# Batched 64x64 matmul: all of `a` loaded as fp32 through SyncE's queue, cast on VectorE

## The chip, the core and the metric

The kernel runs on one core of one Trainium2 chip. The metric is device time in microseconds (us); lower is better. The core has five engines that matter here: TensorE (PE, matrix products and transposes), VectorE (DVE), ScalarE (ACT), GpSimd (POOL) and SyncE (SP, which here only issues transfers). Sixteen DMA engines move data between the chip's memory (HBM) and the on-chip buffer SBUF. They are fed by queues, and three queues carry this kernel's data: `q0` takes what GpSimd issues, `q1` what SyncE issues, `q10` what ScalarE issues.

## The reference

```python
def setup_inputs():
    return {"a": np.random.randn(1024, 64, 64).astype(np.float32),
            "b": np.random.randn(1024, 64, 64).astype(np.float32)}

def reference(a, b):
    return np.matmul(a, b).astype(np.float32)
```

There are 1024 independent products of 64x64 matrices. Each of `a`, `b` and the output is 16 MiB of fp32, so the least traffic to HBM is 48 MiB.

## The kernel before

**Units of work.** The kernel walks over `a` in 8 slabs `s` of 128 matrices (2 MiB each) and over `b` and the output in 16 blocks `t` of 64 matrices (1 MiB each). Slab `s` serves the blocks `t = 2s` and `t = 2s + 1`; two successive blocks are called a pair below.

**What happens to a slab of `a`.** `load_a` brings it in as four quarters `h`, in each of which a partition holds a contiguous run of 1024 numbers (4 KB of fp32 in HBM). In the kernel before, quarters 0 to 2 go through GpSimd's queue, which turns them into bf16 on the way (the tile `a_sb` is bf16). Quarter 3 goes through SyncE's queue as fp32 into `a_raw`. `regroup` then writes one bf16 tile `a_bf`: line 108 reorders the three bf16 quarters, line 111 casts the fp32 one, both on VectorE. Slab 0 is different (`load_first_a`): its quarters are loaded as fp32, two on SyncE and two on ScalarE, into two borrowed output tiles, and cast by VectorE and ScalarE in turn (line 105). `transpose` turns `a_bf` on TensorE, moving pairs of bf16 as one fp32, and ScalarE copies the result into `at_sb` (line 123).

**What happens to a block.** `spread` (line 133) makes four VectorE copies from `at_sb` into a block-diagonal tile `at_bd`. `cast` (line 144) turns `b` into bf16, on VectorE except for block 0 (ScalarE) and the last block (both, lines 149 and 151). `multiply` runs 64 matmuls (line 189), and `evacuate` copies the result from PSUM to `o_sb` (line 177): eight copies on ScalarE for an even block, six on ScalarE and two on VectorE for an odd one. `store` sends the 1 MiB out (line 166), on GpSimd's queue for blocks 0 to 13, on SyncE's and ScalarE's for the last two.

**Order.** The schedule is written by hand; each engine works through its own instructions in the order of the program, and a queue's transfers go in the order of issue. Iteration `t` of the main loop does `spread(t+1)`, `cast(t+1)`, `load_b(t+3)`, for even `t` from 2 to 6 `load_a(t/2+4)`, then `multiply(t)`, and for even `t` the `regroup` of slab `t/2+2`. `load_b` uses SyncE for even blocks and ScalarE for odd ones:

```python
            if t + B_AHEAD < n_t:
                load_b(t + B_AHEAD)
            if half == 0 and 0 < s < n_s - 1 - A_AHEAD:
                load_a(s + 1 + A_AHEAD)
```

Slabs 1 to 4 are requested before or during iteration 0, and slabs 5, 6, 7 in iterations 2, 4 and 6. There are three buffers each for `a_sb`, `a_raw` and `b_sb` (`A_AHEAD`, `B_AHEAD`), so a load waits until the tile three before it has been consumed; there are eight for `o_sb`.

Of the kernel before, what the change touches and what calls it, by code (L numbers as in the profile page):

```python
# [8 lines left out]
fp32 = mybir.dt.float32  # L9
bf16 = mybir.dt.bfloat16  # L10
# [3 lines left out]
def kernel(  # L14
# [14 lines left out]
    nc = tc.nc  # L29
    B, M, K = a.shape  # L30
    _, _, N = b.shape
# [8 lines left out]
    a_v = a.rearrange("(s g h) (mp v) k -> s h g mp (v k)", h=4, g=32, v=16)  # L40
# [4 lines left out]
    a_pool = ctx.enter_context(tc.tile_pool(name="a_pool", bufs=A_AHEAD))  # L45
    b_pool = ctx.enter_context(tc.tile_pool(name="b_pool", bufs=B_AHEAD))
    work = ctx.enter_context(tc.tile_pool(name="work", bufs=2))
    o_pool = ctx.enter_context(tc.tile_pool(name="o_pool", bufs=8))
    t_psum = ctx.enter_context(
        tc.tile_pool(name="t_psum", bufs=4, space=bass.MemoryType.PSUM)  # L50
    )
# [9 lines left out]
    a_tiles, b_tiles, abf_tiles, at_tiles, bbf_tiles = {}, {}, {}, {}, {}  # L61
# [6 lines left out]

    def load_a(s):

        a_sb = a_pool.tile([128, 3, 16, 64], bf16, name="a_sb")
        for h in range(3):
            nc.gpsimd.dma_start(  # L73
                out=a_sb[:, h, :, :].rearrange("p v k -> p (v k)"), in_=a_v[s, h], single_packet=True
            )
        a_raw = a_pool.tile([128, 16, 64], fp32, name="a_raw")
        nc.sync.dma_start(out=a_raw[:].rearrange("p v k -> p (v k)"), in_=a_v[s, 3])  # L77
        a_tiles[s] = a_sb, a_raw

    def load_first_a():  # L80

        raw = [
            o_pool.tile([128, 8, 2, 2, 64], fp32, name="o_sb")[:].rearrange(
                "p gh j wl n -> p (gh j wl n)"
            )
            for _ in range(2)
        ]
        parts = [raw[h % 2][:, 1024 * (h // 2) : 1024 * (h // 2) + 1024] for h in range(4)]
        for h in range(4):
            (nc.scalar if h % 2 else nc.sync).dma_start(out=parts[h], in_=a_v[0, h])  # L90
        a_tiles[0] = parts

    def load_b(t):
        b_sb = b_pool.tile([128, 16, 128], fp32, name="b_sb")
        queue = nc.scalar if t % 2 else nc.sync
        queue.dma_start(out=b_sb[:], in_=b_v[t])  # L96
        b_tiles[t] = b_sb

    def regroup(s):
        a_sb = a_tiles.pop(s)  # L100
        a_bf = work.tile([128, 16, 4, 64], bf16, name="a_bf")
        if s == 0:
            for h in range(4):
                copy = nc.scalar.copy if h % 2 else nc.vector.tensor_copy
                copy(a_bf[:, :, h, :], a_sb[h].rearrange("p (v k) -> p v k", v=16))  # L105
        else:
            cast_sb, raw = a_sb
            nc.vector.tensor_copy(  # L108
                a_bf[:, :, 0:3, :], cast_sb[:].rearrange("p h v k -> p v h k")
            )  # L110
            nc.vector.tensor_copy(a_bf[:, :, 3, :], raw[:])  # L111
        abf_tiles[s] = a_bf
        at_tiles[s] = work.tile([128, 2, 32, 2, 4, 4], fp32, name="at_sb")

    def transpose(s, j):
        a_cols = abf_tiles[s][:].rearrange("p v h k -> p v (h k)").bitcast(fp32)
        for wl in range(2):
            at_ps = t_psum.tile([128, 4, 128], fp32, name="at_ps")
            for vo in range(4):
                nc.tensor.transpose(  # L120
                    at_ps[:, vo, :], a_cols[:, 4 * vo + 2 * j + wl, :], identity[:]
                )
            nc.scalar.copy(  # L123
                at_tiles[s][:, j, :, wl, :, :],
                at_ps[:].rearrange("p vo (g mp) -> p g mp vo", mp=4),
            )

    def spread(t):
        half = slice(16 * (t % 2), 16 * (t % 2) + 16)
        bd = bd_tiles[t % N_BD]  # L130
        for h in range(4):
            rows = slice(32 * h, 32 * h + 32)
            nc.vector.tensor_copy(  # L133
                bd[rows, :, :, :, h, :].rearrange("p j g wl mo -> p j (g wl) mo"),
                at_tiles[t // 2][rows, :, half, :, :, :].rearrange(
                    "p j g wl mp vo -> p j (g wl) (mp vo)"
                ),
            )

    def cast(t):  # L140
        b_bf = work.tile([128, 16, 128], bf16, name="b_bf")
        b_sb = b_tiles.pop(t)
        if t < n_t - 1:
            (nc.vector.tensor_copy if t else nc.scalar.copy)(b_bf[:], b_sb[:])  # L144
        else:
            for gq in range(4):
                rows = slice(4 * gq, 4 * gq + 4)
                if gq % 2:
                    nc.vector.tensor_copy(b_bf[:, rows, :], b_sb[:, rows, :])
                else:  # L150
                    nc.scalar.copy(b_bf[:, rows, :], b_sb[:, rows, :])  # L151
        bbf_tiles[t] = b_bf

    def store(t):
        for piece in held.pop(t):
            piece()
# [51 lines left out]
            held[t] = [lambda q=q: put(q, 8 if whole else 4) for q in ([0] if whole else [0, 4])]  # L208

    with tc.manual_schedule():  # L210
        load_first_a()

        nc.vector.memset(warm[:, 0:1], 0.0)
        nc.scalar.copy(warm[:, 1:2], warm[:, 0:1])  # L214
        load_b(0)
        load_b(1)
        nc.vector.memset(bd_tiles[0][:], 0.0)  # L217
        make_identity(nc, identity)
        nc.gpsimd.memset(bd_tiles[1][:, 0], 0.0)
        load_a(1)  # L220
        load_b(2)
        nc.gpsimd.memset(bd_tiles[1][:, 1], 0.0)
        load_a(2)
        regroup(0)
        transpose(0, 0)
        transpose(0, 1)
        spread(0)
        cast(0)
        for t in range(n_t):
            s, half = t // 2, t % 2  # L230
            if t + 1 < n_t:
                spread(t + 1)
                cast(t + 1)
# [4 lines that stand above are left out]
            if half == 0 and 0 < s < n_s - 1:  # L238
                transpose(s + 1, 1)
            multiply(t)  # L240
            if t == 0:
                regroup(1)
                load_a(A_AHEAD)
                load_a(A_AHEAD + 1)
                transpose(1, 0)
                transpose(1, 1)
            elif t == 1:
                regroup(2)
            elif half == 0 and s + 2 < n_s:
                regroup(s + 2)  # L250
            if half == 1 and s + 2 < n_s:
                transpose(s + 2, 0)
            if t >= HOLD - 1:
                store(t - HOLD + 1)
        for t in range(n_t - HOLD + 1, n_t):
            store(t)
# [30 lines left out]
```

## Time and profile before

| | |
|---|---|
| runs, median (lowest to highest) | 135.07 us (134.95 to 135.22), 3 runs |
| profiled execution: span from its first to its last instruction | 133.4 us |
| what lies around the span (median less span) | 1.7 us |
| VectorE busy | 94.6 us, 71% |
| ScalarE busy | 87.9 us, 66% |
| TensorE busy (matmul) | 64.4 us, 48% |
| GpSimd busy | 33.0 us, 25% |
| HBM read and written | 33.55 + 16.78 MB, 377 GB/s over the span |

The profiled execution has no separate clocking; its own time is its span of 133.4 us and the 1.7 us around it that the runs show. The profile gives busy times per engine, the span cut into 40 equal slices, the load of each DMA queue, the chain of work that ended last (followed back from the last instruction), and groups of instructions by source line with their number, busy time and mean duration. The GB/s of the DMA views count bytes as they are written at the destination: a quarter that is turned into bf16 on the way counts half of what was read for it. The last line of the table counts the bytes at HBM.

### The profile page before, as it was taken

What the parts mean: (1) busy time and instruction counts of PE and PEld (TensorE: products, weight loads), DVE (VectorE), ACT (ScalarE), POOL (GpSimd) and SP (SyncE); (2) the same over time, 40 slices, a digit from 0 to 9 for tenths busy, and PEclk for the clock granted to TensorE, in tenths of its full rate; (3) what the DMA queues carried; (4) which work ended last, traced back from release to release, by engine and by line L of the source; (5) the groups of instructions that cost most, each with busy time, mean ns of one, the idle gap of its engine ahead of it and who ended that gap; (6) DMA issues with size and microseconds to landing.
All of it is one profiled execution on the core that took longest, in us unless ns stands there. A gap on an engine that the chain in (4) does not pass through costs nothing.

```text
span 133.4 us, 2837 instructions
## 1 busy us (share of the span) xinstructions
PE 64.4 (48%) x1152; PEld 61.1 (46%) x1152; DVE 94.6 (71%) x120; ACT 87.9 (66%) x161; POOL 33.0 (25%) x43
## 2 busy tenths in 40 slices
PE   0006406960089384289518970956197363970000
PEld 0006306950089274189418950945196363960000
DVE  5930399109998809995999699959999995987000
ACT  3225424999036998969595969696968969099600
POOL 8991000420090070341233021203020410300000
PEclk9999975797557999856985699599959955599555
DMA  3999999999999999999999999999999999999990
GB/s 77 371 329 311 307 311 281 284 306 325 327 312 401 316 320 333 399 384 397 311 281 375 406 389 351 304 316 390 394 396 387 396 392 391 402 405 398 382 319 18
DMA packets 19021, 45.01 MB, mean 337 GB/s; under 512 B 1088, under 2 KB 3136, under 8 KB 19008
## 3 DMA queue, kind: packets, MB, share of 16 engines
q0 software_dynamic: 6832, 20.19, 50.1%
q1 hardware_dynamic: 7120, 14.68, 30.4%
q10 hardware_dynamic: 5056, 9.96, 19.7%
q8 instruction: 9, 0.15, 0.4%
q14 instruction: 4, 0.03, 0.1%
HBM read 33.55 MB, written 16.78 MB: 377 GB/s over the span
## 4 chain that ended last, share of the span: by engine, by line
DMA 53%; DVE 15%; ACT 13%; PE 6%; issue 5%; SPq 2%; DVEq 0%; ACTq 0%
DMA b_sb<-in_b_dram 53%; ACT o_sb L177 9%; DVE at_bd L133 6%; PE o_ps L189 4%; DVE b_bf L144 4%; DVE o_sb L177 3%; PE at_ps L120 2%; ACT at_sb L123 2%; ACT b_bf L144 1%; SPq L90 1%; DVE a_bf L108 1%; SPq L96 1%; ACT b_bf L151 1%; DVE a_bf L111 0%; SPq L77 0%
## 5 line engine op out<-in xcount | busy, mean ns | idle before, releaser
L177 ACT COPY o_sb<-o_ps 64x512 f32<-64x512 f32 x106 | 61.5, 580 | 10.3 <-PE o_ps L189 9.0
L189 PEld LDWEIGHTS <-at_bd 128*128 128x128 bf16 x1024 | 42.3, 113 | 39.5 <-DVE b_bf L144 25.7
L189 PE MATMUL o_ps<-b_bf,at_bd 128*128 128x64 bf16 x960 | 42.6, 216 | 35.4 <-DVE b_bf L144 23.4
L133 DVE COPY at_bd<-at_sb 32x1024 f32<-32x1024 f32 x64 | 46.9, 733 | 14.1 <-ACT at_sb L123 11.8
L120 PE MATMUL at_ps<-identity,a_bf 128*128 128x128 f32 x128 | 21.2, 335 | 19.4 <-ACT a_bf L105 11.2
L166 POOL DMA_DIRECT2D out_dram<-o_sb x14 | 15.4, 1097 | 56.9 <-ACT at_sb L123 23.4
L120 PEld LDWEIGHTS at_ps<-identity,a_bf 128*128 128x128 f32 x128 | 19.3, 180 | 19.5 <-issue 19.5
L123 ACT COPY at_sb<-at_ps 128x512 f32<-128x512 f32 x32 | 17.5, 590 | 11.0 <-PE at_ps L120 7.8
L144 DVE CAST b_bf<-b_sb 128x2048 bf16<-128x2048 f32 x14 | 17.8, 1271 | 9.6 <-DMA b_sb<-in_b_dram 9.4
L73 POOL DMA_DIRECT2D a_sb<-in_a_dram x21 | 13.6, 662 | 26.4 <-DVE a_bf L108 19.4
L177 DVE COPY o_sb<-o_ps 64x512 f32<-64x512 f32 x14 | 9.7, 690 | 0.3
L108 DVE COPY a_bf<-a_sb 128x3072 bf16<-128x3072 bf16 x7 | 6.7, 950 | 0.0
L105 ACT CAST a_bf<-o_sb 128x1024 bf16<-128x1024 f32 x2 | 2.1, 1044 | 5.2 <-DMA o_sb<-in_a_dram 5.2
L111 DVE CAST a_bf<-a_raw 128x1024 bf16<-128x1024 f32 x7 | 4.8, 683 | 0.0
L144 ACT CAST b_bf<-b_sb 128x2048 bf16<-128x2048 f32 x1 | 1.9, 1900 | 3.9 <-DMA b_sb<-in_b_dram 3.9
L105 DVE CAST a_bf<-o_sb 128x1024 bf16<-128x1024 f32 x2 | 2.8, 1382 | 1.9 <-DMA o_sb<-in_a_dram 1.9
L217 DVE MEMSET at_bd<- 128x4096 f32 x1 | 3.5, 3472 | 0.8 <-issue 0.8
L177 DVE COPY o_sb<-at_ps 64x256 f32<-64x256 f32 x8 | 3.4, 422 | 0.5 <-PE at_ps L189 0.4
L151 ACT CAST b_bf<-b_sb 128x512 bf16<-128x512 f32 x2 | 1.1, 615 | 3.6 <-DMA b_sb<-in_b_dram 3.6
L177 ACT COPY o_sb<-at_ps 64x256 f32<-64x256 f32 x8 | 2.9, 366 | 0.1
L214 ACT ACT_TABLE_LOAD x1 | 1.3, 1283 | 2.3 <-issue 2.3
L189 PE MATMUL at_ps<-b_bf,at_bd 128*128 128x64 bf16 x64 | 2.0, 193 | 1.0 <-DVE at_bd L133 1.0
(12 smaller groups left out, 6.1 us busy)
## 6 DMA issues: line engine op xcount, KB each, us to landing
out_dram<-o_sb POOLq DMA_DIRECT2D x14, 1024.0 KB, 21.6
a_sb<-in_a_dram POOLq DMA_DIRECT2D x21, 256.0 KB, 16.4
a_raw<-in_a_dram SPq DMA_DIRECT2D x7, 512.0 KB, 18.7
o_sb<-in_a_dram SPq DMA_DIRECT2D x2, 512.0 KB, 5.9
o_sb<-in_a_dram ACTq DMA_DIRECT2D x2, 512.0 KB, 7.1
out_dram<-o_sb SPq DMA_DIRECT2D x2, 512.0 KB, 7.5
out_dram<-o_sb SPq DMA_DIRECT2D x2, 256.0 KB, 7.8
out_dram<-o_sb ACTq DMA_DIRECT2D x2, 256.0 KB, 5.5
```

What stands on the lines that cost most here:

```text
L73: nc.gpsimd.dma_start(out=a_sb[:, h, :, :].rearrange("p v k -> p (v k)"), in_=a_v[s, h], single_packet=True)
L105: copy(a_bf[:, :, h, :], a_sb[h].rearrange("p (v k) -> p v k", v=16))
L108: nc.vector.tensor_copy(a_bf[:, :, 0:3, :], cast_sb[:].rearrange("p h v k -> p v h k"))
L111: nc.vector.tensor_copy(a_bf[:, :, 3, :], raw[:])
L120: nc.tensor.transpose(at_ps[:, vo, :], a_cols[:, 4 * vo + 2 * j + wl, :], identity[:])
L123: nc.scalar.copy(at_tiles[s][:, j, :, wl, :, :], at_ps[:].rearrange("p vo (g mp) -> p g mp vo", mp=4),)
L133: nc.vector.tensor_copy(bd[rows, :, :, :, h, :].rearrange("p j g wl mo -> p j (g wl) mo"), at_tiles[t // 2][rows, :, half, :, :, :].rearrange(
L144: (nc.vector.tensor_copy if t else nc.scalar.copy)(b_bf[:], b_sb[:])
L166: store_queue(t, lo).dma_start(out=o_v[t, :, lo : lo + n, :], in_=o_sb[:, lo : lo + n].rearrange("p gh j wl n -> p (gh j wl n)"),)
L177: copies[2 * par + wl](dst, src)
L189: nc.tensor.matmul(o_ps[:, gl, g % 2, j, :], at_bd[:, j, g, :, u], b_bf[:, g, 64 * u : 64 * u + 64], start=(u == 0), stop=(u == 1),)
L217: nc.vector.memset(bd_tiles[0][:], 0.0)
```

## The change

All four quarters of every slab are loaded as fp32 into one tile of 4 x 16 x 64 numbers per partition. SyncE issues all of them, except that for slab 0 the odd quarters stay with ScalarE. Slab 0 uses the same pool of three buffers as the others instead of borrowed output tiles. `regroup` of slabs 1 to 7 is one VectorE instruction that reorders and casts 4096 numbers per partition; slab 0 is cast as it was. GpSimd issues stores alone. As the tile of `a` grows from 10 KB to 16 KB per partition, the output pool goes from eight buffers to seven.

```diff
-    o_pool = ctx.enter_context(tc.tile_pool(name="o_pool", bufs=8))
+    o_pool = ctx.enter_context(tc.tile_pool(name="o_pool", bufs=7))
...
     def load_a(s):
 
-        a_sb = a_pool.tile([128, 3, 16, 64], bf16, name="a_sb")
-        for h in range(3):
-            nc.gpsimd.dma_start(
-                out=a_sb[:, h, :, :].rearrange("p v k -> p (v k)"), in_=a_v[s, h], single_packet=True
-            )
-        a_raw = a_pool.tile([128, 16, 64], fp32, name="a_raw")
-        nc.sync.dma_start(out=a_raw[:].rearrange("p v k -> p (v k)"), in_=a_v[s, 3])
-        a_tiles[s] = a_sb, a_raw
-
-    def load_first_a():
...
-        for h in range(4):
-            (nc.scalar if h % 2 else nc.sync).dma_start(out=parts[h], in_=a_v[0, h])
-        a_tiles[0] = parts
+        a_sb = a_pool.tile([128, 4, 16, 64], fp32, name="a_sb")
+        for h in range(4):
+            queue = nc.scalar if s == 0 and h % 2 else nc.sync
+            queue.dma_start(out=a_sb[:, h, :, :].rearrange("p v k -> p (v k)"), in_=a_v[s, h])
+        a_tiles[s] = a_sb
...
-                copy(a_bf[:, :, h, :], a_sb[h].rearrange("p (v k) -> p v k", v=16))
+                copy(a_bf[:, :, h, :], a_sb[:, h, :, :])
         else:
-            cast_sb, raw = a_sb
-            nc.vector.tensor_copy(
-                a_bf[:, :, 0:3, :], cast_sb[:].rearrange("p h v k -> p v h k")
-            )
-            nc.vector.tensor_copy(a_bf[:, :, 3, :], raw[:])
+            nc.vector.tensor_copy(a_bf[:], a_sb[:].rearrange("p h v k -> p v h k"))
...
-        load_first_a()
+        load_a(0)
```

More of the change, by code (lines that the diff above doesn't have):

```diff
@@ L69, in load_a @@
     def load_a(s):
-        a_sb = a_pool.tile([128, 3, 16, 64], bf16, name="a_sb")
-        for h in range(3):
-            nc.gpsimd.dma_start(
-                out=a_sb[:, h, :, :].rearrange("p v k -> p (v k)"), in_=a_v[s, h], single_packet=True
-            )
-        a_raw = a_pool.tile([128, 16, 64], fp32, name="a_raw")
-        nc.sync.dma_start(out=a_raw[:].rearrange("p v k -> p (v k)"), in_=a_v[s, 3])
-        a_tiles[s] = a_sb, a_raw
-    def load_first_a():
-        raw = [
-            o_pool.tile([128, 8, 2, 2, 64], fp32, name="o_sb")[:].rearrange(
-                "p gh j wl n -> p (gh j wl n)"
-            )
-            for _ in range(2)
-        ]
-        parts = [raw[h % 2][:, 1024 * (h // 2) : 1024 * (h // 2) + 1024] for h in range(4)]
+        a_sb = a_pool.tile([128, 4, 16, 64], fp32, name="a_sb")
         for h in range(4):
-            (nc.scalar if h % 2 else nc.sync).dma_start(out=parts[h], in_=a_v[0, h])
-        a_tiles[0] = parts
+            queue = nc.scalar if s == 0 and h % 2 else nc.sync
+            queue.dma_start(out=a_sb[:, h, :, :].rearrange("p v k -> p (v k)"), in_=a_v[s, h])
+        a_tiles[s] = a_sb
     def load_b(t):
@@ L104, in regroup @@
                 copy = nc.scalar.copy if h % 2 else nc.vector.tensor_copy
-                copy(a_bf[:, :, h, :], a_sb[h].rearrange("p (v k) -> p v k", v=16))
+                copy(a_bf[:, :, h, :], a_sb[:, h, :, :])
         else:
-            cast_sb, raw = a_sb
-            nc.vector.tensor_copy(
-                a_bf[:, :, 0:3, :], cast_sb[:].rearrange("p h v k -> p v h k")
-            )
-            nc.vector.tensor_copy(a_bf[:, :, 3, :], raw[:])
+            nc.vector.tensor_copy(a_bf[:], a_sb[:].rearrange("p h v k -> p v h k"))
         abf_tiles[s] = a_bf
```

## The prediction

> **What bounds the kernel now.** I read the page's slices and queues first, then the chain, then the DMA view of two windows, then VectorE's timeline.
>
> ```profile
> DMA  3999999999999999999999999999999999999990
> GB/s 77 371 329 311 307 311 281 284 306 325 327 312 401 316 320 333 399 384 397 311 281 375 406 389 351 304 316 390 394 396 387 396 392 391 402 405 398 382 319 18
> ...
> HBM read 33.55 MB, written 16.78 MB: 377 GB/s over the span
> ...
> DMA 53%; DVE 15%; ACT 13%; PE 6%; issue 5%; SPq 2%; DVEq 0%; ACTq 0%
> ```
>
> The DMA engines are full from the second slice to the last but one, no compute engine is (VectorE 71%), and over half of the chain that ended last is loads of `b`. The GB/s dip to 300 only where casting loads run, as their bytes count half. The DMA view from 0 to 89 us, when the load of block 10 of `b` has just landed, shows this:
>
> ```profile
> q0 software_dynamic: 4337, 10.68, 47.4%
> q1 hardware_dynamic: 4535, 11.16, 34.8%
> q10 hardware_dynamic: 3328, 7.11, 20.9%
> ```
>
> The columns are packets, MB written and share. A casting packet writes 2 KB for 4 KB read and a store's carries 4 KB. Some 26 transfers had finished on q0, each with 16 marker packets, so about 3920 packets hold 10.68 MB: 2630 casting (10.3 MiB read) and 1290 store packets (5.0 MiB). q1 holds 4.5 MiB of fp32 `a` (two quarters of slab 0, seven `a_raw`) and 6.1 MiB of `b`; q10 holds 1 MiB of `a` and 5.8 of `b`. That makes `a` 15.8, `b` 11.9, stores 5.0: 32.7 MiB in HBM bytes. Transfers start near 2.4 us, so a MiB takes (89 - 2.4)/32.7 = 2.65 us, whatever the mixture: from 100 to 111 us, without any `a`, 4.32 MB written take 11 us, or 2.67 us per MiB. **Rule A: N MiB have moved at 2.4 + 2.65 N.** All 48 give 129.6 us; the present kernel's transfers end near 131. So at most 1.5 us can be won, and order is all the change can spoil.
>
> GpSimd had issued nine stores by 89 us (the ninth at 84.2) and five MiB had landed. The page says the same:
>
> ```profile
> out_dram<-o_sb POOLq DMA_DIRECT2D x14, 1024.0 KB, 21.6
> ```
>
> A store needs 21.6 us to land because it shares q0 with the casting loads. **Four MiB of stores stand aside while loads pass, and are paid at the end, beside the last blocks' computing.** How queues share is in the DMA view from 100 to 111 us, where all three have work nearly throughout:
>
> ```profile
> q0 software_dynamic: 608, 2.34, 55.2%
> q1 hardware_dynamic: 525, 1.04, 24.8%
> q10 hardware_dynamic: 463, 0.92, 22.6%
> ```
>
> Packets come out nearly one for one; with 4 KB packets on q0 and 2 KB of `b` on the others, q0 gets over half of the bytes. Last, VectorE's timeline over one pair and the end:
>
> ```profile
> 83.10 0.95 DVE L108 COPY a_bf<-a_sb 128x3072 bf16<-128x3072 bf16 x1
> 83.97 0.68 DVE L111 CAST a_bf<-a_raw 128x1024 bf16<-128x1024 f32 x1
> ...
> 89.08 1.23 DVE L144 CAST b_bf<-b_sb 128x2048 bf16<-128x2048 f32 x1 [1.31 <-DMA b_sb<-in_b_dram]
> ...
> 96.02 0.95 DVE L108 COPY a_bf<-a_sb 128x3072 bf16<-128x3072 bf16 x1
> ...
> 112.33 1.23 DVE L144 CAST b_bf<-b_sb 128x2048 bf16<-128x2048 f32 x1 [1.47 <-DMA b_sb<-in_b_dram]
> ...
> 115.01 3.09 DVE L133 COPY at_bd<-at_sb 32x1024 f32<-32x1024 f32 x4
> ```
>
> A pair takes 96.02 - 83.10 = 12.9 us, of which VectorE waits 1.3 for an even block of `b` (SyncE's). It is nearly full where it matters, though 71% overall.
>
> **The change, part by part.**
>
> *Regroup.* Before: 22.32 to 23.87 us, 1.55 us for both lines. After: one cast of 4096 numbers. L144 takes 1.23 us for 2048, L111 0.68 for 1024, hence 2.45 to 2.75; L108 shows that the reordered reading is not slower, so I take 2.5: +0.95 us a slab, 6.7 us over seven. Six fall where VectorE waits for `b` anyway (below); slab 7's lies on the end.
>
> *GpSimd.* 21 issues (13.6 us) go. GpSimd is 25% busy, so this is worth nothing itself. Ten of the 16 groups of four `at_bd` copies take 3.1 to 3.2 us rather than 2.83; all ten overlap store issues, which stay. One output buffer less: bound by stores in flight, which become fewer; 0.
>
> *Bytes.* HBM bytes stay. Rule A held at 2.65 with casting and 2.67 without, so fp32 may cost 0.02 x 10.5 MiB = 0.2 us, at most; 0.
>
> *Start.* Before, the first block of `b` lands at 19.26 us, behind casting loads. After, only 2 MiB of slab 0 and block 1 share with it: 2.4 + 4 x 2.65 = 13. The first product moves from 21.2 to about 16.5 us (spread(0), now 15.45 to 18.3, ends some 1.8 earlier as slab 0 arrives without competition). That is no gain at the end, since rule A governs the next arrivals; it makes stores start earlier.
>
> *Queues: the main term.* SyncE now issues 28 quarters instead of 7 for slabs 1 to 7, and its queue is a line: slab 4 stands ahead of block 4 of `b`, slab 5 ahead of 6, slab 6 ahead of 8, slab 7 ahead of 10. SyncE also waits for a free `a` buffer with the next even `b` behind it, but these buffers (slab 7 needs regroup(4), near 57 us) are free before the line gets there. Stores have q0 alone. With 4 KB packets on q0 and q1 and 2 KB on q10 their turn is 4/10 of the bytes; a pair needs 2 MiB of stores out of 6, 33%. So stores no longer fall behind; each goes out soon after it is made, in front of loads that computing waits for.
>
> Block 4 of `b` lands when slabs 0 to 4 (10), blocks 0 to 4 (5), some 0.7 of block 5 and the first 2.7 stores have moved: 18.4 MiB, 51.2 us; before 50.2. From there each pair must move all its 6 MiB, 15.9 us, where VectorE needs 12.9 - 1.3 + 0.95 = 12.6: the loads set the pace, three pairs 47.7 us. Block 10 lands at **98.9**. Counted directly: 16 of `a`, 11.8 of `b`, S stores. Nine stores exist by then, and the newest is in part still waiting: S = 8.5, N = 36.3, **X = 98.6** against 89.1. Bounds of S: 5.0 (as before) and 9: X from 89.3 to 99.9.
>
> *From X to the end.* cast(10) to the end of the last spread was 118.10 - 89.08 = 29.0 us; less the wait of 1.47, plus 0.95, 28.5. ScalarE then had waited until 116.88 for block 15 of `b` and so began block 14's copies at 118.04 (4.73 us), the last eight until 125.85, last issue, landing 5.5, end 133.4. After X only 11.7 MiB remain (31 us), so block 15 is there in time: cast(14) ends at X + 24.0, half its product 1.8 later, 4.73 + 3.06 of copies: last issue X + 33.6 to 34. Landing, on emptier queues, 4.3 (the shortest that the trace has for these tiles) to 5.5; I take 4.3, then 2.05 to the end as before: X + 40.3. If block 15 is late it is X + 43.8, the old 44.3 less 0.5.
>
> Sum: 98.6 + 40.3 = 138.9 of span, 5.5 over 133.4; with 1.65 around it 140.5, rounded to **140.3 us**.
>
> The Trainium skill, page "DMA: Bandwidth & Descriptors", section "Issuing engines are not separate DMA queues", says that transfers issued by any engine run on the same 16 DMA engines and interleave, so that choosing among issuers saves only issue time. Rule A agrees for the total, and by this rule alone the sum would be 135.07 us; the 21.6 us landing shows that the order is not indifferent, and I go by the row.
>
> **Rivals.** *The lag of stores persists* (for: q0 has been slow throughout; against: the casting loads explain it). With S = 5, X stays at 89.3, waits of 1.1 to 1.5 us per pair swallow the longer regroup, and the end moves by 0 to 0.9: 135.1 to 136.
>
> *Faster.* Place: the turns between SyncE's and GpSimd's queues. If SyncE's gets well over one packet for one against a software queue, loads overtake stores, the 4.7 us earlier start is kept and the end is shorter. It decides where X + 40.3 < 133.4, so X < 93.1, at most 6.4 stores landed. Then rule A's floor rules: 129.6 + 2 to 3 of end, 133.3 to 134.3 in time. For: b at 13 us, 21 software issues gone. Against: the one-for-one packets.
>
> That the change does less than it says: only slab 0 is untouched, and that is in the counts.
>
> **Numbers.** Forecast 0.76 (bounds S = 7 with the short end 136.3, S = 9 with the long one 145.3), lagging stores 0.10 (0.04 of it no change), faster 0.14. A measurement here can tell 0.2%, 0.27 us, from no change. Slower 0.82, same 0.04, faster 0.14. Range 135.2 to 143.6: it leaves out the faster case and the upper corner.
>
> **What would show it.** Right: stores landing in under 10 us; VectorE's waits for even `b` of several us each between 51 and 99 us; cast(10) near 98; DMA slices below 9 in the last quarter; one 128x4096 cast of 2.5 us, seven times. Wrong: stores still over 15 us to landing, waits for `b` under 2 us, DMA full to the end. If q1 alone doesn't fill the DMA engines, it is worse than said.

## The result and the profile after

| | before | after |
|---|---|---|
| runs, median (lowest to highest) | 135.01 us (134.88 to 135.22), 4 runs | 148.80 us (148.23 to 149.84), 4 runs |
| ratio to before, 95% interval | | 1.103 (1.099 to 1.107) |
| span of the profiled execution | 133.4 us | 146.5 us |
| VectorE busy | 94.6 us | 98.0 us |
| GpSimd busy | 33.0 us | 21.8 us |

The change makes the kernel 13.8 us slower. The forecast was 140.3 us, at most 143.6: the direction was right and the size was not. The lines of the page of the changed kernel that answer to those of before are its slices, two of its queues (packets, MB, share), its HBM line and the landing of GpSimd's stores.

```profile
DMA  3999999999999999999999999999999999982992
GB/s 93 397 329 291 383 364 290 348 399 416 416 414 396 332 296 402 420 313 347 406 413 387 364 388 407 417 315 331 388 395 312 380 351 352 371 304 98 334 341 93
...
q1 hardware_dynamic: 10144, 25.69, 49.4%
q0 software_dynamic: 3808, 14.68, 26.1%
...
HBM read 33.55 MB, written 16.78 MB: 344 GB/s over the span
...
out_dram<-o_sb POOLq DMA_DIRECT2D x14, 1024.0 KB, 10.7
```

The DMA engines are again busy nearly to the end, yet move 344 instead of 377 GB/s. In the kernel before, slices near 300 GB/s were casting loads whose bytes count half. Here nothing is counted half, and 290 means 290. Stores land after 10.7 us instead of 21.6. VectorE's timeline shows its waits for even blocks of `b` (start, duration, in brackets the wait before it); in order they are blocks 4, 6, 8 and 10:

```profile
58.31 1.23 DVE L124 CAST b_bf<-b_sb 128x2048 bf16<-128x2048 f32 x1 [8.55 <-DMA b_sb<-in_b_dram]
...
73.10 1.23 DVE L124 CAST b_bf<-b_sb 128x2048 bf16<-128x2048 f32 x1 [2.44 <-DMA b_sb<-in_b_dram]
...
91.70 1.23 DVE L124 CAST b_bf<-b_sb 128x2048 bf16<-128x2048 f32 x1 [6.37 <-DMA b_sb<-in_b_dram]
...
105.56 1.23 DVE L124 CAST b_bf<-b_sb 128x2048 bf16<-128x2048 f32 x1 [1.51 <-DMA b_sb<-in_b_dram]
```

Block 10 is cast at 105.6 us, against 89.1 before and 98.6 forecast. From there to the end of the span it is 40.9 us (forecast 40.3). So 7.0 of the missing 8.5 us are lost before block 10, and as many already before block 4 (58.3 us against a forecast of 51.2): the three pairs between them took 47.2 us, where 47.7 were forecast.

One place where they are lost is in the DMA view from 10.5 to 15 us, when blocks 0 and 1 of `b` are all that moves:

```profile
DMA packets 643, 1.31 MB, mean 292 GB/s; under 512 B 13, under 2 KB 13, under 8 KB 643
...
q1 hardware_dynamic: 321, 0.66, 52.9%
q10 hardware_dynamic: 322, 0.66, 52.8%
```

At 292 GB/s a MiB takes 3.6 us, not 2.65. Counted from the packets of the trace, 36.1 MiB had moved at 105.5 us: `a` 16.0, `b` 12.2, stores 8.0. By the forecast's rule A they would have moved by 98.1 us. The amounts were right (36.3 forecast, with 8.5 stores); the price of a MiB was not. The good match of the three pairs is in part luck: from 58.3 to 105.5 us only 16.9 MiB moved, not the 18 of the forecast, at 2.8 us each.

How the queues take turns shows from 81.5 to 89.5 us, when all three have work (packets, MB, share):

```profile
q0 software_dynamic: 379, 1.49, 48.5%
q1 hardware_dynamic: 389, 0.86, 28.2%
q10 hardware_dynamic: 376, 0.75, 25.6%
```

Packet for packet they are even, and the stores on `q0`, with the larger packets, take about half of the bytes.

### The profile page after: what moved, and what is told of

Same layout as the page of the kernel before. It is cut to its first block, busy times and chain, and to the rows that moved or that the text cites. A ratio compares the mean times of both kernels' runs of the same rounds, so it can differ in the third digit from the quotient of the medians.

```text
span 146.5 us, 2829 instructions
## 1 busy us (share of the span) xinstructions
PE 71.1 (49%) x1152; PEld 67.9 (46%) x1152; DVE 98.0 (67%) x113; ACT 88.6 (60%) x161; POOL 21.8 (15%) x22
## 4 chain that ended last, share of the span: by engine, by line
DMA 54%; DVE 21%; PE 9%; SPq 4%; ACT 3%; issue 3%; DVEq 0%
DMA b_sb<-in_b_dram 45%; DVE at_bd L113 10%; DMA a_sb<-in_a_dram 9%; PE o_ps L169 8%; DVE o_sb L157 5%; DVE b_bf L124 4%; SPq L74 4%; DVE a_bf L91 2%; ACT o_sb L157 2%; ACT b_bf L124 1%; PE at_ps L169 1%; SPq L80 1%; DVEq L262 0%; DVEq L113 0%; DVEq L91 0%
## 5 line engine op out<-in xcount | busy, mean ns | idle before, releaser
L169 PEld LDWEIGHTS <-at_bd 128*128 128x128 bf16 x1024 | 48.0, 121 | 46.7 <-DVE b_bf L124 36.6
L169 PE MATMUL o_ps<-b_bf,at_bd 128*128 128x64 bf16 x960 | 46.6, 225 | 42.7 <-DVE b_bf L124 34.6
L146 POOL DMA_DIRECT2D out_dram<-o_sb x14 | 17.6, 1256 | 111.5 <-ACT o_sb L157 53.5
L100 PE MATMUL at_ps<-identity,a_bf 128*128 128x128 f32 x128 | 22.1, 346 | 23.8 <-DVE a_bf L91 12.8
L100 PEld LDWEIGHTS at_ps<-identity,a_bf 128*128 128x128 f32 x128 | 20.2, 186 | 24.0 <-issue 24.0
L91 DVE CAST a_bf<-a_sb 128x4096 bf16<-128x4096 f32 x7 | 16.0, 2289 | 4.4 <-DMA a_sb<-in_a_dram 4.4
L80 ACT MOVE_SHAPE b_sb<-in_b_dram x8 | 0.5, 64 | 16.9 <-DVE b_bf L124 13.5
L89 ACT CAST a_bf<-a_sb 128x1024 bf16<-128x1024 f32 x2 | 2.1, 1044 | 5.0 <-DMA a_sb<-in_a_dram 5.0
L169 PE MATMUL at_ps<-b_bf,at_bd 128*128 128x64 bf16 x64 | 3.6, 242 | 1.2 <-DVE at_bd L113 1.2
L89 DVE CAST a_bf<-a_sb 128x1024 bf16<-128x1024 f32 x2 | 1.4, 694 | 2.8 <-DMA a_sb<-in_a_dram 2.8
L199 POOL MEMSET at_bd<- 128x2048 f32 x1 | 1.8, 1799 | 0.0
L202 POOL MEMSET at_bd<- 128x2048 f32 x1 | 1.8, 1799 | 0.0
## 6 DMA issues: line engine op xcount, KB each, us to landing
out_dram<-o_sb POOLq DMA_DIRECT2D x14, 1024.0 KB, 10.7
b_sb<-in_b_dram ACTq DMA_DIRECT2D x8, 0.5 KB, 13.8
```

Of the source, the lines that this page charges most:

```text
L89: copy(a_bf[:, :, h, :], a_sb[:, h, :, :])
L91: nc.vector.tensor_copy(a_bf[:], a_sb[:].rearrange("p h v k -> p v h k"))
L100: nc.tensor.transpose(at_ps[:, vo, :], a_cols[:, 4 * vo + 2 * j + wl, :], identity[:])
L146: store_queue(t, lo).dma_start(out=o_v[t, :, lo : lo + n, :], in_=o_sb[:, lo : lo + n].rearrange("p gh j wl n -> p (gh j wl n)"),)
L169: nc.tensor.matmul(o_ps[:, gl, g % 2, j, :], at_bd[:, j, g, :, u], b_bf[:, g, 64 * u : 64 * u + 64], start=(u == 0), stop=(u == 1),)
```

## The experiments

Two theories came out of this reading, and they need not exclude each other; both were tried below. **Rate:** `b` is read in runs of 512 bytes (pieces that lie together in HBM), which is slow unless something else overlaps with it; casting loads do, fp32 loads don't. **Order:** stores overtake loads that computing waits for, as forecast. The rivals were VectorE's longer cast and SyncE's queue being unable to keep the DMA engines busy.

### Rates measured by themselves

A program that only moves data, in seven stages (it and the next one were run once each):

> This run computes nothing: it moves blocks in seven stages, one after the other, and its output is not the product. Stages: 8 MiB of b in 512-byte runs on SyncE's and ScalarE's queues; 8 MiB of b on ScalarE's alone; 8 MiB of a in 4 KB runs on SyncE's alone; 4 MiB of a (SyncE) beside 4 MiB of b (ScalarE); 4 MiB of b on both beside 4 MiB of stores (GpSimd); 8 MiB of b in 2 KB runs on both; 4 MiB of b on both beside 4 MiB of casting loads (GpSimd). Theory (b in 512-byte runs is slow when nothing with longer runs moves beside it): 3.4 to 3.6 us per MiB in stages 1 and 2 (27 to 29 us each), 2.5 to 2.65 in stages 3 and 6 (20 to 21 us), 2.65 to 2.9 in stages 4, 5 and 7. Rival (SyncE's queue alone cannot keep the DMA engines busy): stage 3 slower than 3 us per MiB, stage 1 not slower than stage 4.

Windows inside the stages, in their order (the last two columns are the DMA engines' busy share and GB/s written):

```profile
4.00:30.00 26.00, 5.40 (x1) 0.81 (x2) 0.00 (x0) 1.00 1.06 293
34.00:62.00 28.00, 0.00 (x0) 2.23 (x6) 0.00 (x0) 1.00 1.04 288
66.00:85.50 19.50, 0.00 (x0) 0.00 (x0) 0.00 (x0) 1.00 1.00 395
90.00:106.00 16.00, 0.00 (x0) 0.66 (x2) 0.00 (x0) 1.00 1.03 351
117.00:138.00 21.00, 0.00 (x0) 0.00 (x0) 2.27 (x3) 1.00 1.02 369
144.00:165.00 21.00, 0.00 (x0) 0.00 (x0) 0.00 (x0) 1.00 1.03 379
170.00:187.00 17.00, 0.00 (x0) 0.00 (x0) 2.19 (x5) 1.00 1.08 305
```

`b` in 512-byte runs moves at 288 to 293 GB/s whether one queue or two carry it, fp32 `a` on SyncE's queue alone at 395, and `b` in 2 KB runs at 379. SyncE's queue can therefore fill the DMA engines, and that rival is out. In stage 4 the view by queues gives 3.34 MB of `a` and 2.28 MB of `b` in 16 us; at their own rates they take 3.34/0.395 + 2.28/0.290 = 16.3 us one after the other, so next to nothing overlaps. In stage 5, 3.58 MB of stores and 4.17 MB of `b` took 21 us. `b` alone would take 14.4, which leaves 6.6 us for the stores, or 540 GB/s, more than any stage moved: stores overlap in part (stores alone were not measured). In stage 7, casting loads wrote 1.57 MB, which is 3.14 MB read, beside 3.60 MB of `b`: 6.74 MB in 17 us, 396 GB/s at HBM. The queues' rows for stages 4 and 7 (`q1` carries `a` in the first and half of `b` in the second):

```profile
q1 hardware_dynamic: 911, 3.34, 60.7%
q10 hardware_dynamic: 1147, 2.28, 42.3%
...
q0 software_dynamic: 862, 1.57, 48.9%
q1 hardware_dynamic: 946, 1.90, 32.6%
q10 hardware_dynamic: 848, 1.70, 26.4%
```

Per MiB these are 3.6 us in stages 1 and 2, 2.65 in stage 3, 3.0 in stage 4, 2.8 in stages 5 and 6 and 2.65 in stage 7 (in bytes at HBM). Stages 4 and 6 are slower than I had expected.

Stage 4 and stage 7 differ in the issuing queue too, so the second program put both kinds of loads on GpSimd's:

> This run computes nothing; its output is not the product. Four stages: 4 MiB of b in 512-byte runs on SyncE's and ScalarE's queues beside 4 MiB of a as fp32 on GpSimd's; the same beside 4 MiB of a that GpSimd's queue casts to bf16; 4 MiB of b in 2 KB runs beside 4 MiB of fp32 a on GpSimd's; 4 MiB of casting loads alone. From the run before: b alone 3.6 us per MiB, fp32 a alone 2.55, b beside casting loads 2.57 on the whole. Theory (a casting load overlaps with 512-byte runs and an fp32 load does not): 3.0 to 3.1 us per MiB in stage 1, where the sum of both alone is 3.08, and 2.5 to 2.6 in stage 2; 2.6 in stage 3. Rival (any load on GpSimd's queue overlaps): 2.6 in stage 1 as in stage 2.

```profile
5.00:23.00 18.00, 4.40 (x1) 0.00 (x0) 0.66 (x2) 1.00 1.04 339
31.00:47.00 16.00, 0.00 (x0) 0.00 (x0) 1.67 (x4) 1.00 1.08 306
56.00:72.00 16.00, 0.00 (x0) 0.00 (x0) 1.02 (x2) 1.00 1.04 395
79.00:89.00 10.00, 0.00 (x0) 0.00 (x0) 2.39 (x5) 1.00 1.10 202
```

Beside fp32 loads on GpSimd's queue: 339 GB/s, 3.09 us per MiB, the sum of both alone as expected. Beside casting loads: 306 written, and with 1.46 of 4.89 MB written by casts (twice that read) 396 GB/s at HBM, 2.65 us per MiB; I had said 2.5 to 2.6. With 2 KB runs fp32 loads cost nothing extra (395). Casting loads alone read 404 GB/s. So the overlap does not belong to the queue: it comes with the casting loads. One thing is not separated. The casting loads are issued with the option `single_packet=True`, as in the kernel before, and none of the fp32 loads is, here or in any run below. The number of packets doesn't differ (`q0` has 6832 in the kernel before and in the next experiment), but no run has the option without the cast or the cast without it. Where casting is named as the cause below, cast and option together are meant.

### Undoing the queue

```diff
-            queue = nc.scalar if s == 0 and h % 2 else nc.sync
+            if s == 0:
+                queue = nc.scalar if h % 2 else nc.sync
+            else:
+                queue = nc.gpsimd if h < 3 else nc.sync
```

> The changed kernel with one thing undone: quarters 0 to 2 of slabs 1 to 7 go back to GpSimd's queue, still as fp32, and VectorE still casts all four. Theory (the queue is the cause, through the order and through what runs beside b): 135 to 137 us. Rival (VectorE's longer cast or the fp32 bytes in SBUF are the cause): 143 to 149 us.

Measured: 142.05 us, ratio to before 1.051 (1.047 to 1.054). It fell between the two expectations. The edit doesn't bring back the option `single_packet=True`. The stores are slow to land again:

```profile
out_dram<-o_sb POOLq DMA_DIRECT2D x14, 1024.0 KB, 21.9
```

Half of the loss (6.8 us) goes away with the queue, and 7.0 us stay though the stores fall behind as before. What stays is fp32 instead of casting loads: the rate, VectorE's cast, or both.

### Longer runs of `b`

```diff
-    b_v = b.rearrange("(t g h) (kp u) n -> t (h kp) g (u n)", h=4, g=16, u=2)
+    b_v = b.rearrange("(t c pa) (pb x) n -> t (pa pb) c (x n)", c=4, pa=16, x=8)
...
-        queue.dma_start(out=b_sb[:], in_=b_v[t])
+        queue.dma_start(
+            out=b_sb[:].rearrange("p (c y) n -> p c (y n)", c=4), in_=b_v[t]
+        )
```

These kernels multiply other rows of `b` and serve for the time alone. In the changed kernel:

> The changed kernel with b read in runs of 2 KB instead of 512 bytes (the rows land in other places, so the products are of other data). Packets stay 2 KB, so the turns between the queues stay. Theory (some 7 us of the loss are slow 512-byte runs that meet only each other, the other 5.5 to 7 are the order): 140.5 to 142.5 us, with DMA rates of 2.5 to 2.7 us per MiB up to 100 us. Rival (all of the loss is order or SyncE's queue): 147.5 to 149 us.

Measured: 141.98 us, ratio 1.045 (1.040 to 1.049), as the theory had it. Its slices show the lost rate back, up to about 100 us:

```profile
GB/s 75 397 331 407 413 392 394 407 408 411 415 412 411 397 407 413 406 392 411 420 407 403 411 411 412 401 401 404 374 284 393 305 311 401 282 169 141 335 339 89
```

Block 10 is now cast at 99.58 us, within 1 us of the forecast's 98.6, and the rest of the span takes 40.8 us. The forecast's 140.3 us is nearer to the time of this kernel than to that of the changed one.

In the kernel before, as a control:

> The kernel before with b read in runs of 2 KB, as a control. Theory: there other transfers with longer runs nearly always move beside b, so little is to be had: 133.5 to 135.2 us. Rival (512-byte runs cost the same in both kernels): 127 to 130 us.

Measured: 133.68 us, ratio 0.990 (0.987 to 0.994). The 512-byte runs cost 1.4 us there and 6.8 us in the changed kernel.

With the queue undone as well:

> The changed kernel with both suspects undone: quarters 0 to 2 of slabs 1 to 7 on GpSimd's queue as fp32, and b read in 2 KB runs (products of other data). What is left of the change is VectorE's one cast of 2.3 us per slab, the fp32 bytes and the buffers. Theory (order plus slow 512-byte runs are all of it): 133.5 to 135.5 us, as the kernel before with 2 KB runs (133.7). Rival (the longer cast costs by itself, 0.7 us a slab): 137 to 140 us.

Measured: 133.29 us, ratio 0.987 (0.984 to 0.990), 0.2 us under the theory's range. VectorE's longer cast, the fp32 bytes and the seven buffers cost nothing here. The four kernels with all of `a` in fp32, and the two of before, make a table (us):

| | `b` in 512-byte runs | `b` in 2 KB runs |
|---|---|---|
| three quarters cast on GpSimd's queue (before) | 135.0 | 133.7 |
| the same quarters as fp32 on GpSimd's queue | 142.05 | 133.3 |
| all on SyncE's queue (the change) | 148.8 | 142.0 |

Down the left column, the loss of the cast costs 7.0 us and the move to SyncE 6.8. Down the right, the loss of the cast costs nothing (133.3 against 133.7) and the move 8.7.

### How much is cast

Quarters cast on GpSimd's queue, from one to four. One:

```diff
-        a_sb = a_pool.tile([128, 3, 16, 64], bf16, name="a_sb")
-        for h in range(3):
...
+        a_sb = a_pool.tile([128, 16, 64], bf16, name="a_sb")
...
+        a_raw = a_pool.tile([128, 3, 16, 64], fp32, name="a_raw")
+        for h in range(1, 4):
+            (nc.gpsimd if h < 3 else nc.sync).dma_start(
+                out=a_raw[:, h - 1, :, :].rearrange("p v k -> p (v k)"), in_=a_v[s, h]
+            )
```

> The kernel before with one quarter of slabs 1 to 7 cast on GpSimd's queue instead of three; two more go through the same queue as fp32, the fourth through SyncE's as ever; seven output buffers. Known: three quarters cast 135.0, none 142.05. Theory (each MiB loaded with a cast overlaps with 512-byte runs and saves about 7.0/10.5 = 0.67 us against fp32): 3.5 MiB cast give 139.7, 139 to 140.5 us. Rival (having the cast at all or not, for instance the buffers or GpSimd's descriptors, makes the difference): below 137 or above 141.5 us.

Measured: 138.96 us, ratio 1.031 (1.029 to 1.033), a hair under the expected range. Four:

```diff
-        a_sb = a_pool.tile([128, 3, 16, 64], bf16, name="a_sb")
-        for h in range(3):
+        a_sb = a_pool.tile([128, 4, 16, 64], bf16, name="a_sb")
+        for h in range(4):
```

> The step the other way: the kernel before with the fourth quarter of slabs 1 to 7 also cast on GpSimd's queue, regroup one bf16 copy. Theory (transfers full at 2.65 us per MiB already, casting loads overlap with the 512-byte runs, fp32 loads do not): 3.5 MiB of fp32 loads become overlapping ones, worth at most 0.5 us each MiB, and the end moves only if block 15 comes earlier: 133.3 to 135.2 us. Rival (the queue of GpSimd is overloaded by four quarters and slabs come late): 136 to 139 us.

Measured: 134.87 us in 12 runs, ratio 0.998 (0.997 to 0.9995). None, one, three and four quarters give 142.05, 138.96, 135.0 and 134.87 us. The first 3.5 MiB save 3.1 us, the next 7 MiB 4.0, the last 3.5 MiB 0.1 to 0.2. The gain is graded, as the rate theory has it, and runs out at the kernel whose transfers are at 2.65 us per MiB already. This is the fastest kernel of the study that forms the same products, by a margin that hardly counts.

### Holding the stores back

```diff
-    HOLD = 2
+    HOLD = 5
...
-    def store(t):
+    def store(t, after=None):
+        if after is not None:
+            nc.gpsimd.tensor_copy(gate[:], bbf_tiles[after][:, 0, 0:1])
...
-                store(t - HOLD + 1)
+                store(t - HOLD + 1, t + 1 if t + 1 < n_t else None)
```

> The changed kernel with GpSimd's stores held back: store(t-4) is issued only when block t+1 of b has been cast (one tiny GpSimd copy of a column of the cast tile ahead of each). Theory (stores overtake the loads that computing waits for): block 10 of b lands 6 to 9 us earlier, at 97 to 100 us, the end pays some of it back: 141 to 146 us. Rival (stores do not matter, only the slabs ahead of b in SyncE's line, or only the rate): 148 to 151 us.

Measured: 147.61 us, ratio 1.093 (1.090 to 1.096); between the two expectations. VectorE's timeline and the slices show a half of it that held:

```profile
96.19 1.23 DVE L124 CAST b_bf<-b_sb 128x2048 bf16<-128x2048 f32 x1 [0.99 <-DMA b_sb<-in_b_dram]
...
127.86 3.48 DVE L161 COPY o_sb<-at_ps 64x256 f32<-64x256 f32 x8 [1.19 <-PE at_ps L173]
...
DMA  3999999999999999999999999999999999999994
```

Block 10 is cast 9.4 us earlier, a little more than the expected 6 to 9, and VectorE's last copies end at 131.3 instead of 140.5 us. But now the DMA engines are busy into the last slice: the stores that were held back go out after the computing, and the span is only 1.1 us shorter (145.4 against 146.5).

To see the order without the rate, the same holding was tried with `b` in 2 KB runs:

> The changed kernel with stores held back as in the earlier run and b in 2 KB runs (products of other data), so that the transfers as a whole are no longer slow and only the order is left to see. Theory (stores overtake loads, and that is the whole of the 8.3 us by which the change is slower with 2 KB runs): 133.5 to 137 us against 142.0 without the holding, waits of VectorE for even blocks under 3 us each. Rival (even blocks are late because slabs stand ahead of them in SyncE's line, whatever the stores do): 140 to 142 us.

Measured: 142.48 us, ratio 1.051 (1.046 to 1.056), 0.5 us above the rival's range. Block 10 was cast at 91.3 us (99.6 without holding) and VectorE ended at 126.2 instead of 134.6, but held stores left the DMA engines short of work (from 92 to 94 us, and not yet at 88 as the next expectation has it, they were busy for 43% and moved 94 GB/s), and what was left went out after the computing. So the time speaks for the rival and the trace for the theory. The last run holds only stores 0 to 5:

> As the run before with stores held and b in 2 KB runs (products of other data), but only stores 0 to 5 are held, each until block t+5 is cast; from store 6 on they go as soon as they are made. The run before cast block 10 at 91.3 us instead of 99.6 and ended computing at 126.2 instead of 134.6, but left the DMA engines partly idle from 88 us on and the stores for the end. Theory (order: stores overtook loads that computing waits for; the long holding then only starved the end): computing ends near 126 as there, the span near 133 to 135: 134 to 137 us. Rival (stores held back cost at the end whatever they give before): 140 to 143 us.

Measured: 137.99 us, ratio 1.025 (1.019 to 1.030); 1.0 us above the theory's range; 4.0 us of the 8.3 come back (142.0 to 138.0). Its last copies and its slices:

```profile
123.45 3.49 DVE L163 COPY o_sb<-at_ps 64x256 f32<-64x256 f32 x8 [1.19 <-PE at_ps L175]
...
GB/s 86 390 311 404 410 399 389 404 408 408 408 405 393 395 403 388 393 407 406 403 414 411 414 412 408 407 400 155 331 415 362 398 379 411 405 406 358 337 349 136
```

Computing ends at 126.9 us, 7.6 earlier than with stores unheld (134.6). The slice at 155 GB/s, near 92 us, is a gap of some 2 us in which loads had run out and the next stores still waited for block 10. The rival that holding only costs is refuted; that order is the whole of the 8.3 us is not shown, since this clumsy holding gave back half in time. A rival for the rest stands untested: in the changed kernel SyncE's queue had packets almost without a gap until 112 us, while ScalarE's had none for about 42 of the first 106. Slabs shared between these two queues were not tried.

### Slabs requested later

```diff
-            if half == 0 and 0 < s < n_s - 1 - A_AHEAD:
-                load_a(s + 1 + A_AHEAD)
+            if half == 0 and 0 < s < n_s - A_AHEAD:
+                load_a(s + A_AHEAD)
...
-                load_a(A_AHEAD + 1)
```

> The changed kernel with slabs 4 to 7 requested two blocks later each, so that every even block of b from 4 on stands behind one slab less in SyncE's line. Theory of order: 2 MiB less ahead of block 10 are 5.3 us: 142 to 146 us, unless regroup starts to wait for its slab. Rival (the rate is all): 148 to 150 us.

Measured: 149.58 us, ratio 1.108 (1.104 to 1.112). The exception in the expectation came true: block 10 was cast at 100.6 us, 4.9 earlier than in the changed kernel and near the 5.3 of the theory, but then the waits moved from `b` to the slabs, and block 12 was cast 2.0 us later (119.9 against 117.9).

```profile
92.98 2.29 DVE L91 CAST a_bf<-a_sb 128x4096 bf16<-128x4096 f32 x1 [1.72 <-DMA a_sb<-in_a_dram]
...
111.24 2.29 DVE L91 CAST a_bf<-a_sb 128x4096 bf16<-128x4096 f32 x1 [3.57 <-DMA a_sb<-in_a_dram]
```

Here, moving one load ahead of another in the same line gained nothing at the end, as both were needed at the same pace; of what was tried within the changed order, only deferring what nobody waits for, the stores, brought the end of the computing forward.

## Why the prediction was right or wrong

**The direction, and the order term: right in the main.** The forecast put the loss into loads in SyncE's line that wait while stores go out at once. Stores landed after 10.7 us (forecast: under 10, against 21.6 before), the stores done at block 10 were 8.0 MiB (8.5), and the move of the queue alone costs 6.8 us, or 8.7 with 2 KB runs; the forecast's 5.5 us were a little small. How much of it the stores cause is open; holding them gave 4.0 us back, with 2 KB runs. Of the waits for even blocks, forecast at several us each, two were long (8.55 and 6.37) and two short.

**From block 10 to the end: right, with luck in the parts.** It took 40.9 us against 40.3, and block 15 was there in time, as forecast. But the last store was issued 35.1 us after block 10's load (forecast 33.6 to 34), and the 4.3 us for its landing was misread: the shortest store of the trace of before took 5.4, and 4.3 belongs to a load into an output tile. In the changed kernel the shortest store took 4.8.

**The step that failed is rule A, "whatever the mixture", and with it that fp32 may cost at most 0.2 us.** I took 2.65 us per MiB from two windows of the kernel before, one with casting loads and stores beside `b` and one with stores beside `b`. Both are mixtures that overlap with 512-byte runs, the second in part. The changed kernel has long stretches of the mixtures that don't: `b` with `b` at 3.6 us per MiB, `b` with fp32 `a` at the sum of both. Up to block 10 its transfers took 2.85 us per MiB on average (103.1 us for 36.1 MiB). In the table this term is 7.0 us; the forecast had 0. I read no window of the trace of before with `b` alone or with fp32 loads alone beside it, so the price was unknown, and I should have bounded it instead of carrying the rate over.

The DMA engines' busy share gave no warning. In the windows by stage of the trace of before it is the last column but one:

```profile
20.00:25.00 5.00, 3.76 (x67) 3.76 (x67) 3.81 (x5) 3.04 (x6) 1.43 (x3) 0.51 1.08 275
...
110.00:115.00 5.00, 2.79 (x54) 2.64 (x52) 3.46 (x4) 3.21 (x6) 0.36 (x1) 0.50 1.03 394
```

With casting loads it was 1.08, with stores 1.03. But the program of the rates has 1.06 for `b` alone, which is slow, and 1.02 for `b` beside stores, which overlap in part: the share says that the engines are full, and not how fast a mixture moves.

**VectorE's cast: right that it costs next to nothing.** Its length was 2.29 us (2.5 forecast), and 133.3 against 133.7 us with 2 KB runs leaves no price, not even the 0.95 us that the forecast charged at the end for slab 7.

**The earlier start: right that it is worth nothing.** The first block was cast at 16.1 us instead of 19.3 (forecast: landed at 13; from 10.5 us on `b` moved alone, at 292 GB/s). Block 4 came at 58.3 us all the same.

**The rivals.** That the stores keep lagging was wrong, and so was the faster case: SyncE's queue got no more than its turn (379, 389 and 376 packets on the three queues from 81.5 to 89.5 us). The Trainium skill, page "DMA: Bandwidth & Descriptors", section "Issuing engines are not separate DMA queues", says that starting transfers on several engines saves only the time it takes to start them. The time of this kernel goes further: with the same fp32 bytes, the choice of the issuer was worth 6.8 us.

## What to carry to other kernels

A rate read from a trace belongs to the mixture of transfers that it was read in; before it is carried over to a changed kernel, ask which transfers will move beside each other there, and bound the rate where the trace has no such window. Where the DMA engines are full, work that nobody waits for (stores) is worth keeping behind loads, and a shared queue may be doing that by accident. A casting load, issued as it was here, that looks like a burden on GpSimd may be what hides the short runs of another load.

## What the runs showed of the hardware

- Loads in 512-byte runs moved at 288 to 293 GB/s, on one queue or on two; in 2 KB runs at 379, fp32 loads in 4 KB runs at 395.
- Beside 512-byte runs, fp32 loads in 4 KB runs overlapped not at all (339 GB/s, the sum of both times), stores in part (369 GB/s), and casting loads so far that the mixture read 396 GB/s. The run lengths were changed together with the places in HBM that a transfer touches, the casting loads alone had the option `single_packet=True`, and why they overlap was not tried: the mechanism stays open.
